# Element-wise work moved from GpSimd to VectorE, operands split in the tile they were loaded into, and one pair's scaled tokens kept, in a hybrid decoder layer

## The chip, the cores and the metric

The kernel runs on one core of a Trainium2 chip. The metric is the device time of one execution in microseconds (us). The kernel before takes 2348.49 us, the median of three runs (2345.11 to 2351.36). TensorE multiplies matrices; VectorE (DVE in the profile), ScalarE (ACT) and GpSimd (POOL) do element-wise work; SP issues nearly all transfers between HBM and the on-chip memory (SBUF). Matmul results lie in PSUM, from where VectorE or ScalarE fetch them.

## The reference

One decoder layer on 2048 tokens of width 1024, all in float32:

```python
h = modulate(rmsnorm(x, norm1_w), shift1, scale1)
x = x + gate1 * hybrid_mixer(h, ...)      # w_in, attention | state space, w_out
h = modulate(rmsnorm(x, norm2_w), shift2, scale2)
g, u = split(h @ w_gate_up)               # width 2816 each
x = x + gate2 * ((silu(g) * u) @ w_down)
return rmsnorm(x, final_norm_w)
```

`hybrid_mixer` is one input projection, then a sliding-window attention (window 128) in 8 heads beside a chunked state-space scan in 8 heads with a causal convolution before and a gated norm behind, and one output projection (`w_out`) of the two side by side. Shifts, scales and gates come from a small product of `c`.

## The kernel before, in words

*Tiling.* Activations lie transposed: features on the 128 partitions, 512 tokens (a block, `T`) along the free dimension; there are four blocks, `b` = 0 to 3. Width 1024 is 8 tiles (`KT`), 2816 is 22 (`NF`) or, in halves, 11 (`KP`).

*Two halves of every operand.* Matmuls take a 32-bit format that keeps fewer bits of the mantissa. So each operand is split: ScalarE copies it to the rounded form (`hi`), and VectorE or GpSimd subtracts that from the original (`lo`). A product is then three matmuls, hi by hi, hi by lo and lo by hi. That makes a subtraction of 128x512 elements for every weight tile and every token tile, the commonest element-wise work of the kernel. `weight` (L260) does it for projections, with an argument for the engine; `halves` (L849) for the gate and up weights; `shifted` and `kept` (L875, L880) for tokens of the feed-forward part; `tokens_of` (L1055) and the steps of `steps_of` (L1066) for the down projection. The last two alternate between VectorE and GpSimd, by counters.

*Stages.* (1) For each block: norm, projections, convolution, attention (`attentions`) and scan (`ssds`), with an output projection (`out_proj`, L808) at its end. It reads the block's eight mixed tiles, which attention and scan have left in HBM (`spill`): `mixed` (L802) loads each into a temporary tile `t` and splits it into an operand pair. Chunk c of the projection takes 24 matmuls into one PSUM bank; then L821 adds the gated result to x, which frees the bank for chunk c + 2. The projections of blocks 2 and 3 run after the first `quads`.

(2) The feed-forward part works on pairs of blocks, `s` = 0 and 1. Gate and up products are done with seven block products in place of eight: `quad` (L956) makes, from four loaded weight tiles, four sums and differences s1 to s4 (L962 to L968), splits seven weights, and multiplies them by seven prepared token operands (b11, b21, t1, b22, t3, t2, t4); some twenty adds and multiplies on the results follow, and the products go to HBM. One `quad` is 84 matmuls, and there are 22 for each `s`. `operands_last` (L930) prepares the token operands of the second pair: four tiles per k are loaded, scaled (`scaled`, L865, with its operation at L872) and combined.

(3) The down projection uses the same scheme: seven stages per pair (`pairs.stage`), each multiplying eleven token tiles (loaded ahead in a `ring` by `tokens_of`) by four chunks of weights (`steps_of`, 12 steps). Three stages of the first pair run before the second pair's quads. Four of the seven weights are sums of the down weights, made once by `weight_sums` (L1038) in 16 pieces beside the quads: four loads, two operations on VectorE, two on GpSimd, four stores.

*Order.* Every engine works through its queue in order. The program is written as generators that yield between pieces; `beside(main, ratio)` runs side work in a given share. A scheduler then sets each engine's order from a simulated timeline, except where a block fixes it for TensorE (the first part) or VectorE (the last stage). So a small edit of an engine moves neighbours too. `norm_of` issues the final norm of a finished block at steps 2 and 5 of the next stage.

*Tiles.* Split weights have 6 tiles (`SPLIT`), raw ones 5 (`RAW`), temporaries 8 (`TMP`). The eight operand pairs of an output projection, `mo`, come from one pool per block (`op` and `op3`).

Of the kernel before, what the change touches and what calls it, by code (L numbers as in the profile page):

```python
# [43 lines left out]
def hymba_layer(ctx, tc, xT, crow, pos, wada, wadk, vecs, rows, wq, wkv, wz, wx, wo, wgu, wd, outT):  # L44
# [206 lines left out]

    def split(x, into):
        hi, lo = into
        nc.scalar.activation(hi, x, AF.Copy)
        split.last = nc.vector.tensor_tensor(lo, x, hi.bitcast(F32), ALU.subtract)
        return hi, lo
# [545 lines left out]
    def mixed(b, mix, cs, into):  # L802
        for c in cs:
            m = tmp()
            nc.sync.dma_start(m, spill[b][c])
            mix.append(split(m, into(c)))

    def out_proj(b, y_of, mix, bank_of, acc, norm=None, each=lambda c: None):  # L808
        for c in range(KT):
            ps = bank_of(c)  # L810
            for half in range(2):
                if half:
                    yield
                whi, wlo = weight(wo[c, half], T, ("o", c, half), b == 0, nc.gpsimd if half or b < 2 else nc.vector, b > 1)
# [26 lines left out]

    flip = [0]

    def lower(lo, x, hi):
        flip[0] += 1
        eng = nc.vector if flip[0] % 2 else nc.gpsimd
        eng.tensor_tensor(lo, x, hi.bitcast(F32), ALU.subtract)
# [40 lines left out]
    def operands_first(s, ops, bc):  # L888

        for k in range(4):  # L890
            h = scaled(s, k, bc, ((0, 0), (1, 0)))
            shifted(ops["b11"][k], h[0, 0], shift_of(k, 0))
            shifted(ops["b21"][k], h[1, 0], shift_of(k, 1))
            yield

# [34 lines left out]
    def operands_last(s, ops, bc):  # L930

        for k in range(4):
            h = scaled(s, k, bc, ((1, 1), (0, 1), (0, 0), (1, 0)))
# [3 lines left out]
            kept(ops["t3"][k], t3)  # L937
# [4 lines left out]
            kept(ops["t2"][k], t2)  # L942
# [13 lines left out]
    def quad(s, f, ops, banks, fresh, behind):  # L956
# [5 lines left out]
        nc.gpsimd.tensor_tensor(s1, a21, a22, ALU.add)  # L962
        nc.gpsimd.tensor_tensor(s2, s1, a11, ALU.subtract)
        ws1 = halves(s1, nc.vector)
        ws2 = halves(s2, nc.gpsimd)
        nc.gpsimd.tensor_tensor(s3, a11, a21, ALU.subtract)
        ws3 = halves(s3, nc.gpsimd)
        nc.gpsimd.tensor_tensor(s4, a12, s2, ALU.subtract)  # L968
        ws4 = halves(s4, nc.gpsimd)
# [68 lines left out]
    def weight_sums(pool):  # L1038

        n = KP * P // 4  # L1040
        for c in range(4):
            for q in range(4):
# [5 lines left out]
                nc.gpsimd.tensor_tensor(a21, a21, a22, ALU.add)  # L1048
                nc.vector.tensor_tensor(a22, a22, a11, ALU.subtract)
                nc.gpsimd.tensor_tensor(a12, a12, a22, ALU.subtract)  # L1050
# [4 lines left out]
    def tokens_of(s, name, pool, n):  # L1055

        for k in range(KP):
# [4 lines left out]
            flip[0] += 1  # L1062
            (nc.vector if flip[0] % 2 else nc.gpsimd).tensor_tensor(lo, raw, hi.bitcast(F32), ALU.subtract)  # L1063
            yield hi, lo

    def steps_of(act, src, banks, new, done, ts=slice(0, T), kept_w=None):  # L1066

        turn = [0]
        for c in range(4):
# [3 lines left out]
            for lo, hi in CHUNKS:  # L1073
# [3 lines left out]
                else:  # L1077
                    turn[0] += 1
# [10 lines left out]
                    (nc.vector if turn[0] % 2 else nc.gpsimd).tensor_tensor(w[1], raw, w[0].bitcast(F32), ALU.subtract)  # L1089
# [579 lines left out]
```

## Time and profile before

| | value |
|---|---|
| median of three runs | 2348.49 us (2345.11 to 2351.36) |
| profiled execution | 2349.26 us, its span 2347.6 us |
| mean granted TensorE clock | 0.971 |
| matmuls | 11072 |
| element-wise instructions of VectorE and GpSimd | 2674 and 1287 |
| bytes read from HBM and written to it | 335.50 MB and 130.61 MB |

The page gives busy time by engine. "Idle before" in a row of a group is the time the engine stood still just before its instructions, and the name behind it is what ended that. In the waits, "A <- B: total, times, longest" says that A stood still until B was done. PEclk is the share of full clock that TensorE was granted; in stretches in which it idles the clock falls for a while and matmuls last longer, so that time is lost beyond the gap itself. A stretch such as 1240.00:1280.00 is counted from the first instruction. In time, the first part fills about 0 to 780 us, the quads of the first pair 780 to 1320, the output projections of blocks 2 and 3 about 1260 to 1440, three down stages 1440 to 1500 and beyond, the quads of the second pair from 1540, and the other eleven down stages from 1980 to the end.

### The profile page before, as it was taken

To read this page: it belongs to the slowest core of one execution; us is meant where nothing else is said; L and a number is where in the kernel's file an instruction comes from. 1 tells how busy PE (TensorE), PEld (TensorE's weight loads), DVE (VectorE), ACT (ScalarE), POOL (GpSimd) and SP (SyncE) were. 2 spreads that over 40 slices of the span, in tenths; PEclk is the share of its full clock that TensorE was granted. 3 is DMA by queue.
4 is the path that set the end of the run, shared out by engine and by line. 5 is a ranking of instruction groups with operands and counts; after the bars stand their busy time and mean duration, and the time that the engine had idled before them with its cause. 6 is when DMAs were issued, how large, how long until landed. Compare 5 with 4: busy or idle time off the path is not lost. (4 is left out here: it accounts for less than half of the span.)

```text
span 2347.6 us, 33637 instructions
## 1 busy us (share of the span) xinstructions
PE 2194.1 (93%) x11072; PEld 1817.4 (77%) x11072; DVE 1625.4 (69%) x2674; ACT 1006.1 (43%) x2113; POOL 1355.4 (58%) x1287
## 2 busy tenths in 40 slices
PE   6878989999999999999998988998999999999998
PEld 5778778888879788877876766776788888787887
DVE  8987975773568866777774658776766665676565
ACT  4564543654346555333333434442233333544442
POOL 2556433553223845687783636887766665765572
PEclk9998999999999999999998999998999999999999
DMA  8898887777879432433333567766432324867653
GB/s 296 294 325 298 301 255 247 253 248 249 297 265 313 148 100 82 126 99 109 112 113 114 188 219 265 274 217 216 152 108 95 108 95 147 294 228 245 197 178 112
DMA packets 288174, 468.36 MB, mean 200 GB/s; under 512 B 27264, under 2 KB 96896, under 8 KB 288000
## 3 DMA queue, kind: packets, MB, share of 16 engines
q1 hardware_dynamic: 287424, 465.70, 59.4%
q8 instruction: 87, 1.43, 0.3%
q14 instruction: 87, 0.71, 0.1%
q10 hardware_dynamic: 576, 0.52, 0.1%
HBM read 335.50 MB, written 130.61 MB: 199 GB/s over the span
## 5 line engine op out<-in xcount | busy, mean ns | idle before, releaser
L1093 PE MATMUL d<-a,w 128*128 128x512 f32 x1716 | 412.6, 401 | 15.9 <-POOL a L1063 5.2
L1093 PEld LDWEIGHTS d<-a,w 128*128 128x128 f32 x1716 | 326.9, 191 | 98.6 <-POOL a L1063 5.6
L952 PE MATMUL d<-b,w 128*128 128x512 f32 x924 | 367.6, 401 | 7.2 <-ACT t L975 5.8
L954 PE MATMUL d<-b,w 128*128 128x512 f32 x924 | 370.1, 402 | 3.5 <-POOL w L853 2.0
L953 PE MATMUL d<-b,w 128*128 128x512 f32 x924 | 369.5, 400 | 0.3 <-POOL b L883 0.3
L952 PEld LDWEIGHTS d<-b,w 128*128 128x128 f32 x924 | 176.0, 190 | 48.4 <-ACT t L975 6.9
L954 PEld LDWEIGHTS d<-b,w 128*128 128x128 f32 x924 | 175.9, 190 | 44.9 <-POOL w L853 3.2
L852 ACT ACTIVATE w<-s 128x512 fp32r<-128x512 f32 x176 | 110.8, 632 | 226.7 <-PE d L954 167.2
L953 PEld LDWEIGHTS d<-b,w 128*128 128x128 f32 x924 | 176.2, 191 | 40.7 <-POOL b L883 0.7
L853 POOL TENSOR_TENSOR w<-s,w 128x512 fp32r<-128x512 f32 x132 | 190.6, 1446 | 15.7 <-ACT w L852 11.6
L276 PE MATMUL d<-w,hl 128*128 128x256 f32 (+1 forms) x592 | 176.6, 298 | 8.6 <-ACT hl L327 6.4
L278 PE MATMUL d<-w,hl 128*128 128x256 f32 (+1 forms) x592 | 171.9, 290 | 2.0 <-DVE hl L328 2.0
L277 PE MATMUL d<-w,hl 128*128 128x256 f32 (+1 forms) x592 | 171.9, 290 | 0.0
L1089 POOL TENSOR_TENSOR w<-raw,w 128x512 fp32r<-128x512 f32 (+1 forms) x78 | 112.8, 1449 | 86.8 <-ACT w L1088 86.7
L968 POOL TENSOR_TENSOR s<-raw,s 128x512 f32<-128x512 f32 x44 | 58.8, 1337 | 174.3 <-DVE w L853 86.7
L286 POOL TENSOR_TENSOR acc<-acc,t 128x512 f32<-128x512 f32 x70 | 99.2, 1417 | 98.4 <-ACT t L285 98.0
L269 POOL TENSOR_TENSOR w<-raw,w 128x512 fp32r<-128x512 f32 (+1 forms) x68 | 94.7, 1394 | 97.8 <-ACT w L268 89.2
L853 DVE TENSOR_TENSOR w<-raw,w 128x512 fp32r<-128x512 f32 x132 | 138.3, 1050 | 17.7 <-ACT w L852 16.6
L276 PE MATMUL d<-hl,w 128*128 128x512 f32 x352 | 147.2, 418 | 3.2 <-ACT w L268 2.2
L1063 DVE TENSOR_TENSOR a<-a 128x512 fp32r<-128x512 f32 x77 | 104.5, 1372 | 62.7 <-ACT a L1061 56.7
L278 PE MATMUL d<-hl,w 128*128 128x512 f32 x352 | 141.2, 401 | 1.4 <-DVE w L269 0.7
L277 PE MATMUL d<-hl,w 128*128 128x512 f32 x352 | 140.7, 400 | 0.0
(417 smaller groups left out, 5532.0 us busy)
## 6 DMA issues: line engine op xcount, KB each, us to landing
raw<-in_wgu_dram SPq DMA_DIRECT2D x176, 256.0 KB, 2.8
w<-w_x SPq DMA_DIRECT2D x48, 512.0 KB, 5.2
act_t<-t SPq DMA_DIRECT2D x88, 256.0 KB, 2.3
a<-act_t SPq DMA_DIRECT2D x88, 256.0 KB, 5.2
t<-in_xT_dram SPq DMA_DIRECT2D x80, 256.0 KB, 4.1
act_b<-t SPq DMA_DIRECT2D x66, 256.0 KB, 2.1
a<-act_b SPq DMA_DIRECT2D x66, 256.0 KB, 5.1
aw<-in_wada_dram SPq DMA_DIRECT2D x64, 256.0 KB, 4.3
```

What stands on the lines that cost most here:

```text
L276: nc.tensor.matmul(out, ahi, bhi, start=first, stop=False)
L277: nc.tensor.matmul(out, ahi, blo, start=False, stop=False)
L278: mm3.last = nc.tensor.matmul(out, alo, bhi, start=False, stop=last)
L286: eng.tensor_tensor(acc, acc, sq, ALU.add)
L852: nc.scalar.activation(hi, x, AF.Copy)
L853: eng.tensor_tensor(lo, x, hi.bitcast(F32), ALU.subtract)
L952: nc.tensor.matmul(out, ahi, bhi, start=first and k == 0, stop=False, skip_group_check=True)
L953: nc.tensor.matmul(out, ahi, blo, start=False, stop=False, skip_group_check=True)
L954: mm3.last = nc.tensor.matmul(out, alo, bhi, start=False, stop=k == 3, skip_group_check=True)
L1063: (nc.vector if flip[0] % 2 else nc.gpsimd).tensor_tensor(lo, raw, hi.bitcast(F32), ALU.subtract)
L1089: (nc.vector if turn[0] % 2 else nc.gpsimd).tensor_tensor(w[1], raw, w[0].bitcast(F32), ALU.subtract)
L1093: mm3.last = nc.tensor.matmul(ps, w[x][:, ws], act[k][y][:, ts], start=new and k == 0 and x + y == 0, stop=k == KP - 1 and x == 1, skip_gr ...
```

## The change

It has six parts. (a) VectorE takes over from GpSimd: the sums of `quad` (s3 and s4 only for the first pair), all splits of its weights, all splits of tokens and weights in the down projection, the weight sums, the second halves of `wo` in the last two output projections, and two of the four kept operands in `operands_last`. (b) `mixed` loads into the `lo` half of the operand tile and splits there, without a temporary. (c) The operand pairs of blocks 2 and 3 share one ring of 11 tiles; three of block 3's tiles are loaded as block 2's projection nears its end, the other five at the start of block 3's. (d) `operands_first` of the second pair stores its eight scaled tiles in HBM, and `operands_last` loads them instead of loading and scaling again. (e) Tokens for the stage after the last quads are loaded four steps earlier. (f) The final norm is issued at steps 6 and 9.

```diff
     def mixed(b, mix, cs, into):
         for c in cs:
-            m = tmp()
+            hi, lo = into(c)
+            m = lo.bitcast(F32)
             nc.sync.dma_start(m, spill[b][c])
-            mix.append(split(m, into(c)))
+            nc.scalar.activation(hi, m, AF.Copy)
+            nc.vector.tensor_tensor(lo, m, hi.bitcast(F32), ALU.subtract)
+            mix.append((hi, lo))
...
-                whi, wlo = weight(wo[c, half], T, ("o", c, half), b == 0, nc.gpsimd if half or b < 2 else nc.vector, b > 1)
+                whi, wlo = weight(wo[c, half], T, ("o", c, half), b == 0, nc.gpsimd if b < 2 else nc.vector, b > 1)
...
             h = scaled(s, k, bc, ((0, 0), (1, 0)))
+            if s:
+                for i in range(2):
+                    nc.sync.dma_start(scaled_d[i][k], h[i, 0])
...
     def operands_last(s, ops, bc):
...
-            h = scaled(s, k, bc, ((1, 1), (0, 1), (0, 0), (1, 0)))
+            h = {}
+            for i in range(2):
+                h[i, 0] = tmp()
+                nc.sync.dma_start(h[i, 0], scaled_d[i][k])
+            h.update(scaled(s, k, bc, ((1, 1), (0, 1))))
...
-            kept(ops["t3"][k], t3)
+            kept(ops["t3"][k], t3, nc.vector)
...
-            kept(ops["t2"][k], t2)
+            kept(ops["t2"][k], t2, nc.vector)
...
-        nc.gpsimd.tensor_tensor(s1, a21, a22, ALU.add)
-        nc.gpsimd.tensor_tensor(s2, s1, a11, ALU.subtract)
+        nc.vector.tensor_tensor(s1, a21, a22, ALU.add)
+        nc.vector.tensor_tensor(s2, s1, a11, ALU.subtract)
         ws1 = halves(s1, nc.vector)
-        ws2 = halves(s2, nc.gpsimd)
-        nc.gpsimd.tensor_tensor(s3, a11, a21, ALU.subtract)
-        ws3 = halves(s3, nc.gpsimd)
-        nc.gpsimd.tensor_tensor(s4, a12, s2, ALU.subtract)
-        ws4 = halves(s4, nc.gpsimd)
+        ws2 = halves(s2, nc.vector)
+        other = nc.gpsimd if s else nc.vector
+        other.tensor_tensor(s3, a11, a21, ALU.subtract)
+        ws3 = halves(s3, nc.vector)
+        other.tensor_tensor(s4, a12, s2, ALU.subtract)
+        ws4 = halves(s4, nc.vector)
...
-                nc.gpsimd.tensor_tensor(a21, a21, a22, ALU.add)
+                nc.vector.tensor_tensor(a21, a21, a22, ALU.add)
...
-                nc.gpsimd.tensor_tensor(a12, a12, a22, ALU.subtract)
+                nc.vector.tensor_tensor(a12, a12, a22, ALU.subtract)
...
-            (nc.vector if flip[0] % 2 else nc.gpsimd).tensor_tensor(lo, raw, hi.bitcast(F32), ALU.subtract)
+            nc.vector.tensor_tensor(lo, raw, hi.bitcast(F32), ALU.subtract)
...
-                    (nc.vector if turn[0] % 2 else nc.gpsimd).tensor_tensor(w[1], raw, w[0].bitcast(F32), ALU.subtract)
+                    nc.vector.tensor_tensor(w[1], raw, w[0].bitcast(F32), ALU.subtract)
...
-    def loaded(b, c, pool):
-        mixed(b, mixes[b], (c,), lambda c: pair("mo", KT, pool=pool))
+    def loaded(b, c):
+        mixed(b, mixes[b], (c,), lambda c: pair("mo", 11, pool=op))
...
-        yield from output(2)
+        yield from output(2, lambda c: loaded(3, c - 5) if c > 4 else None)
...
-        for c in range(KT):
-            loaded(3, c, op3)
+        for c in range(3, KT):
+            loaded(3, c)
...
-        next(second)
         for i, _ in enumerate(first):
             if i % 2:
                 next(coming, None)
+        next(second)
...
-            if i >= 7 * NF - 12:
+            if i >= 7 * NF - 16:
                 next(coming, None)
...
-                if i in (2, 5):
+                if i in (6, 9):
                     for b in list(finish_of):
                         norm_of(b)
```

The order in which instructions stand moves with it. Lines of the changed kernel are up to ten smaller (L853 becomes L843, L255 becomes L802, L821 becomes L818, L269 becomes L263).

GpSimd's queue at the end of the state-space scan, before. `rss`, `rs` and `ss` belong to the reciprocal root of the scan's gated norm, `s` are weight sums of a quad:

```order
L269 TENSOR_TENSOR w<-raw,w 128x512
L962 TENSOR_TENSOR s<-raw 128x512
L240 TENSOR_SCALAR rss<-ss 128x2
L242 TENSOR_TENSOR rss<-rs 128x2
L963 TENSOR_TENSOR s<-s,raw 128x512
L966 TENSOR_TENSOR s<-raw 128x512
L243 TENSOR_TENSOR rss<-rss 128x2
L244 TENSOR_SCALAR rss<-rss 128x2
L245 TENSOR_TENSOR rs<-rss,rs 128x2
```

and in the change:

```order
L1011 TENSOR_TENSOR t<-t 128x512
L756 TENSOR_TENSOR m_12997<-m_12997,m_12844 128x512
L240 TENSOR_SCALAR rss<-ss 128x2
L242 TENSOR_TENSOR rss<-rs 128x2
L243 TENSOR_TENSOR rss<-rss 128x2
L244 TENSOR_SCALAR rss<-rss 128x2
L1005 TENSOR_TENSOR t<-t 128x512
L245 TENSOR_TENSOR rs<-rss,rs 128x2
```

The sums and a split have left the chain of the root; one addition of a quad's results (L1005) stands in it instead. In TensorE's queue the transposes of that block's result (L715, now L709) stood 5 products behind the last state product and directly ahead of the first `mo` matmul; they now stand 48 products behind the one and 42 ahead of the other.

VectorE's queue at the output projections of blocks 2 and 3, before. `mo` are split mixed tokens, `w` low halves of `wo`, `at` and `am` the two PSUM banks:

```order
L269 TENSOR_TENSOR w<-raw,w 128x512
L255 TENSOR_TENSOR mo<-t,mo 128x512 x3
L269 TENSOR_TENSOR w<-raw,w 128x512
L255 TENSOR_TENSOR mo<-t,mo 128x512 x5
L821 SCALAR_TENSOR_TENSOR t<-at,mod,t 128x512
L821 SCALAR_TENSOR_TENSOR t<-am,mod,t 128x512
```

and in the change, at the last two chunks of block 2:

```order
L818 SCALAR_TENSOR_TENSOR t<-am,mod,t 128x512
L263 TENSOR_TENSOR w<-raw,w 128x512
L802 TENSOR_TENSOR mo<-mo 128x512
L263 TENSOR_TENSOR w<-raw,w 128x512
L818 SCALAR_TENSOR_TENSOR t<-at,mod,t 128x512
L802 TENSOR_TENSOR mo<-mo 128x512
L263 TENSOR_TENSOR w<-raw,w 128x512
L802 TENSOR_TENSOR mo<-mo 128x512 x3
L263 TENSOR_TENSOR w<-raw,w 128x512 x2
```

Eight splits stood ahead of an eviction; five now stand around the last one, and three further up.

VectorE's queue in a quad of the second pair beside the weight sums (`ws`), before:

```order
L1047 TENSOR_TENSOR ws<-ws 128x352
L853 TENSOR_TENSOR w<-s,w 128x512
L1004 TENSOR_TENSOR t<-t,st 128x512
L1049 TENSOR_TENSOR ws<-ws 128x352
L1008 TENSOR_TENSOR t<-t,sm 128x512
L1010 SCALAR_TENSOR_TENSOR t<-t 128x512
```

and in the change:

```order
L1047 TENSOR_TENSOR ws<-ws 128x352
L843 TENSOR_TENSOR w<-s,w 128x512
L1048 TENSOR_TENSOR ws<-ws 128x352
L1004 TENSOR_TENSOR t<-t,st 128x512
L843 TENSOR_TENSOR w<-s,w 128x512
L1049 TENSOR_TENSOR ws<-ws 128x352
L961 TENSOR_TENSOR s<-raw 128x512
L1050 TENSOR_TENSOR ws<-ws 128x352
L843 TENSOR_TENSOR w<-s,w 128x512
L962 TENSOR_TENSOR s<-s,raw 128x512
L1008 TENSOR_TENSOR t<-t,sm 128x512
```

Between the evictions of two products (L1004 and L1008) there stood one sum; now two sums, two splits and two sums of the quad's own stand there.

More of the change, by code (lines that the diff above doesn't have):

```diff
@@ L250, in rsqrt @@
             nc.vector.scalar_tensor_tensor(y, b, 1.5, y, ALU.add, ALU.mult)
[L252 to L256, printed above, removed]
     split_d = {}
@@ L840, in hymba_layer @@
     held = {}
[L842 to L847, printed above, removed]
     def halves(x, eng):
@@ L894, in operands_first @@
             yield
+    scaled_d = [[dr.tile([P, T], F32, name=f"scaled{i}{k}") for k in range(4)] for i in range(2)]
     def operands_between(s, ops, bc):
@@ L1061, in tokens_of @@
             nc.scalar.activation(hi, raw, AF.Copy)
-            flip[0] += 1
-            (nc.vector if flip[0] % 2 else nc.gpsimd).tensor_tensor(lo, raw, hi.bitcast(F32), ALU.subtract)
+            nc.vector.tensor_tensor(lo, raw, hi.bitcast(F32), ALU.subtract)
             yield hi, lo
     def steps_of(act, src, banks, new, done, ts=slice(0, T), kept_w=None):
-        turn = [0]
         for c in range(4):
@@ L1077, in steps_of @@
                 else:
-                    turn[0] += 1
                     n = (hi - lo) * P
@@ L1514, in output @@
         yield from out_proj(b, y_of, mixes[b], lambda c: side_bank(c % 2), sums(op), lambda: side_bank(2), each)
-    def loaded(b, c, pool):
-        mixed(b, mixes[b], (c,), lambda c: pair("mo", KT, pool=pool))
+    def loaded(b, c):
+        mixed(b, mixes[b], (c,), lambda c: pair("mo", 11, pool=op))
     def first_output():
         for c in range(KT):
-            loaded(2, c, op)
+            loaded(2, c)
             if c % 2:
                 yield
-        yield from output(2)
+        yield from output(2, lambda c: loaded(3, c - 5) if c > 4 else None)
     def second_output():
-        for c in range(KT):
-            loaded(3, c, op3)
+        for c in range(3, KT):
+            loaded(3, c)
         yield
@@ L1554, in hymba_layer @@
         act, coming = ring(0, "b11", dn, KP)
-        op3 = outputs.enter_context(tc.tile_pool(name="op3", bufs=1, side="right", reuse_waits="tile"))
         second = second_output()
-        next(second)
         for i, _ in enumerate(first):
```

## The prediction

> **What bounds the kernel now.** I read the first part of the page, the busy times by stretch, the waits of TensorE, and last the order of instructions at the longest waits.
>
> ```profile
> PE 2194.1 (93%) x11072; PEld 1817.4 (77%) x11072; DVE 1625.4 (69%) x2674; ACT 1006.1 (43%) x2113; POOL 1355.4 (58%) x1287
> ```
>
> TensorE is busy for 93%, but not always at full speed. The view by stretches shows where it loses time:
>
> ```profile
> core 0 of [0], span 2347.6 us
> core 0: us, PE busy (x) PEld busy (x) DVE busy (x) ACT busy (x) POOL busy (x), PEclk, DMA share, GB/s
> 780.00:1240.00 460.00, 447.81 (x2159) 366.34 (x2158) 331.30 (x471) 191.43 (x438) 319.91 (x303) 0.99 0.33 106
> 1240.00:1280.00 40.00, 28.97 (x114) 22.78 (x113) 18.58 (x28) 16.66 (x34) 16.47 (x24) 0.83 0.32 95
> 1340.00:1380.00 40.00, 29.25 (x121) 23.23 (x121) 21.12 (x39) 13.65 (x23) 13.99 (x11) 0.87 0.66 221
> 1440.00:1500.00 60.00, 48.22 (x182) 36.67 (x181) 57.33 (x53) 29.76 (x54) 55.29 (x36) 0.89 0.75 256
> 1560.00:1700.00 140.00, 124.64 (x504) 97.91 (x503) 99.15 (x102) 38.09 (x67) 103.13 (x75) 0.94 0.59 187
> 1740.00:1920.00 180.00, 180.00 (x777) 145.85 (x777) 109.16 (x121) 59.63 (x101) 119.48 (x85) 1.00 0.31 103
> 2010.00:2044.00 34.00, 29.86 (x120) 22.93 (x119) 21.67 (x20) 16.05 (x31) 24.52 (x17) 0.95 0.71 245
> 2105.00:2140.00 35.00, 32.34 (x136) 25.66 (x135) 25.11 (x41) 14.65 (x27) 19.74 (x14) 0.95 0.62 197
> ```
>
> The profiled execution took 2349.26 us, its span of 2347.6 and 1.66 around it; the median of the timed runs is 2348.49, near enough that the sum below, made against 2349.3, needs no correction.
>
> From 1740 to 1920 us nothing disturbs TensorE: 777 matmuls in 180 us, 0.2317 us each at clock 1.00. By that pace the other stretches should have taken their count times 0.2317 us. They lose 40 - 26.4 = 13.6 us at 1240; 40 - 28.0 = 12.0 at 1340; 60 - 42.2 = 17.8 at 1440; 140 - 116.8 = 23.2 at 1560; 34 - 27.8 = 6.2 at 2010; and about 4.5 at 2105, where a few of the 136 matmuls are small. That is 77 us, idle time and the slow clock behind it (0.83 at 1240) together. The waits of TensorE from 1240 to 2140 us name the engines in charge (total, times, longest):
>
> ```profile
> PE at L276 <- DVE t L821: 10.2, 1, 10.2
> PE am L954 <- DVE w L853: 7.0, 2, 3.5
> PE st L715 <- ACT m L794: 6.8, 1, 6.8
> PE d L952 <- ACT t L975: 5.8, 2, 4.7
> PE d L1093 <- POOL a L1063: 5.2, 1, 5.2
> PE d L1093 <- DVE w L1089: 4.5, 2, 3.8
> PE am L276 <- ACT mo L254: 4.3, 1, 4.3
> PE sm L291 <- POOL acc L286: 2.7, 1, 2.7
> ```
>
> TensorE mostly waits for low halves and for evictions. From 1440 to 1500 us VectorE (57.33 of 60) and GpSimd (55.29) are both full. And they stretch each other; groups of VectorE from 1740 to 1920 us:
>
> ```profile
> L853 DVE TENSOR_TENSOR w<-raw,w 128x512 fp32r<-128x512 f32 x27 | 27.5, 1017 | 2.2 <-ACT w L852 1.6
> ...
> L1015 DVE TENSOR_TENSOR t<-t 128x512 f32<-128x512 f32 x5 | 8.9, 1784 | 0.0
> L853 DVE TENSOR_TENSOR w<-s,w 128x512 fp32r<-128x512 f32 x10 | 6.9, 689 | 1.6 <-ACT w L852 1.6
> ```
>
> one with an input in PSUM, from 780 to 1240 us, and GpSimd's commonest in the whole span:
>
> ```profile
> L1008 DVE TENSOR_TENSOR t<-t,d 128x512 f32<-128x512 f32 x19 | 13.0, 686 | 28.5 <-PE d L954 28.3
> ```
>
> ```profile
> L853 POOL TENSOR_TENSOR w<-s,w 128x512 fp32r<-128x512 f32 x132 | 190.6, 1446 | 15.7 <-ACT w L852 11.6
> ```
>
> One and the same subtraction takes 0.69 us where it falls clear of GpSimd's work (`w<-s,w`), 1.02 in the mean where it sometimes doesn't, and an operation that always starts beside GpSimd 1.78. One whose second input lies in PSUM (L1008) stays at 0.686. So it is the two inputs from SBUF that collide.
>
> **The change, part by part.** *Moved to VectorE:* by the order, 481 operations leave GpSimd: L853 132, L962 and L963 88, L966 and L968 of the first 22 quads 44, L1089 84, L1063 77, weight sums 32, second halves of `wo` 16, two of the four kept operands 8. At 0.69 us each VectorE gains at most 332 us and loses 8 scalings and part of its stretching; GpSimd loses some 481 x 1.45 = 697. Where TensorE sets the pace, as from 1740 to 1920, this is worth nothing.
>
> *End of the state-space work (1240, 13.6 us).* L715 waits for a scaling by a reciprocal root that GpSimd computes in small operations, with quad work between them:
>
> ```profile
> 1245.13 1.27 POOL L962 TENSOR_TENSOR s<-raw 128x512 f32<-128x512 f32 x1
> 1246.38 0.18 POOL L240 TENSOR_SCALAR rss<-ss 128x2 f32<-128x2 f32 x1
> 1246.72 0.19 POOL L242 TENSOR_TENSOR rss<-rs 128x2 f32<-128x2 f32 x1 [0.16 <-DVE rs L238]
> 1247.08 1.26 POOL L963 TENSOR_TENSOR s<-s,raw 128x512 f32<-128x512 f32 x1 [0.16 <-POOL rss L242]
> 1248.30 1.71 POOL L966 TENSOR_TENSOR s<-raw 128x512 f32<-128x512 f32 x1
> ```
>
> These three big ones, 4.2 us of the 6.8 waited, go. And the changed TensorE order puts 48 products (11 us) ahead of these transposes and 42 behind them, ahead of the first `mo` matmul, which covers the rest and the 4.3 us. Bounds 0 and 13.6; I take 10, near the upper end, since both causes go.
>
> *Fourth block's mixed tokens (1340, 12.0 us).* L821, which frees the PSUM bank, stands in VectorE's queue behind eight splits that wait for loads:
>
> ```profile
> 1352.38 0.69 DVE L255 TENSOR_TENSOR mo<-t,mo 128x512 fp32r<-128x512 f32 x1 [2.21 <-ACT mo L254]
> ...
> 1357.97 0.74 DVE L821 SCALAR_TENSOR_TENSOR t<-at,mod,t 128x512 f32<-128x512 f32 x1
> ```
>
> The loads of these tokens, with their median time to landing:
>
> ```profile
> t<-mix SPq DMA_DIRECT2D x32, 256.0 KB, 5.5
> ```
>
> Now three of the eight are split ahead, and the eviction of the last chunk but one stands before the other five. What is late next: those five reuse tiles of the third block and can only be loaded while its last chunk is multiplied. The first tile is free after 3 of that chunk's 24 matmuls and wanted 9 into the next chunk: 30 x 0.23 = 6.9 us for a landing of 5.5, an ACT pass and a split of 0.69. That is just about even, so a few us of a wait may stay. Bounds 0 and 12; I take 7. For the other blocks, splitting in the loaded tile leaves loads and operations as many as they were, each load only bound to its operand tile: -3 to +3 us, taken as 0.
>
> *Operands of the second pair (1440, 17.8 us).* Of GpSimd's 36 operations there, 28 go: these, with 8 of the 16 L883, and four sums.
>
> ```profile
> L883 POOL TENSOR_TENSOR b<-t,b 128x512 fp32r<-128x512 f32 x16 | 25.5, 1607 | 6.8 <-DMA raw<-in_wd_dram 5.5 <-ACT b L882 1.3
> L1063 POOL TENSOR_TENSOR a<-a 128x512 fp32r<-128x512 f32 x8 | 13.2, 1663 | 0.7 <-ACT a L1061 0.6
> L1089 POOL TENSOR_TENSOR w<-raw,w 128x512 fp32r<-128x512 f32 (+1 forms) x8 | 12.7, 1586 | 0.0
> ```
>
> VectorE's 53 lose 8 scalings, which become loads, and gain 28: 73 x 0.69 = 50 us, against 57 now; TensorE needs 42. Unless work slides to the neighbours the stretch shrinks to VectorE's 50, so by 10; bounds 0 and 17.8; I take 9. The eight stores of scaled tokens are new on SP's queue, the eight reads replace eight reads; hidden behind the stages between them, 0. Were one landing exposed, it would be 5.5 by the row above.
>
> *Weight sums (1560, 23.2 us).* The move cuts both ways here. VectorE already waits for their loads (1440 to 1680 us), and what stands behind in its queue waits too:
>
> ```profile
> L1047 DVE TENSOR_TENSOR ws<-ws 128x352 f32<-128x352 f32 x15 | 14.2, 948 | 24.8 <-DMA ws<-in_wd_dram 24.8
> ```
>
> So far GpSimd could go on splitting summed weights meanwhile; now all seven splits of a quad stand in the one queue. Against that, splits and sums shorten toward 0.69 and 0.52, and the sums no longer pass from engine to engine. Weights are made a quad ahead (84 matmuls, 19 us), longer than a landing. Bounds 0 and 23.2; I take 10, below the middle.
>
> *Down stages.* Tokens of the next stage loaded four steps earlier at the end of the quads, and one engine for all low halves: between 0 and 6.2 us at 2010, taken as 3.5. The norm's matmuls, set back from steps 2 and 5 to 6 and 9, stand 28 matmuls (6.5 us) later, more than the 2.7 waited at L291; the clock of 0.95 over 35 us is 1.8 more: 4 of the 4.5 at 2105. The Trainium skill ("TensorE: Matmul & The Clock Gate", section "HAM oscillation — how this bites in real kernels") lets the clock fall only after idle gaps above about 3.4 us; by it this wait would return 2.7 and the sum come to 40.2. The row shows 0.95 around a gap of 2.7, so I keep 4.
>
> *New load in the first quads (780 to 1240):* the four sums and three splits of 19 quads, 133 operations or 92 us, on VectorE's 331 of 460. Part of its stretching goes with them. Bounds: the 12 us of TensorE's idle time there won, or rival 1's 53 lost; I set 2 lost, because its queue keeps slack.
>
> ```profile
> L968 POOL TENSOR_TENSOR s<-raw,s 128x512 f32<-128x512 f32 x19 | 26.1, 1372 | 74.5 <-DVE w L853 37.8 <-issue 36.0 <-POOL s L966 0.7
> ```
>
> Sum: 10 + 7 + 9 + 10 + 3.5 + 4 - 2 = 41.5; 2349.3 - 41.5 = 2307.8, say **2308 us**.
>
> **Rivals.** (1) *VectorE becomes the bound of the first quads, and the kernel is slower.* 331 + 92 = 423 us of 460 if no stretching goes. VectorE also stands idle for 129 us there, 28.3 of them for TensorE at L1008. Were 90 of those kept, 513 us, 53 more than now; with 43.5 won elsewhere the time is 2359. It decides from some 504 us on. Against it: with GpSimd's share more than halved some of the 331 must fall, and part of that idle time is mere lack of work. Chance 0.12. The Trainium skill ("Perfetto Trace Analysis", section "Optimizing Scalar/DVE Operations") speaks for it: it would relieve a saturated DVE by GpSimd, not the reverse, and warns that shifting work between these two may not help, since they share a port. The 1.78 us row bears out the port.
>
> (2) *The waits are only changed.* VectorE, waiting for loads of the sums and of the five mixed tiles, holds up the weights behind them, so that 1340, 1440 and 1560 give a third of their 26: 2349.3 - 8.7 - 10 - 7.5 + 2 = 2325. For it: the 24.8 us above. Chance 0.20.
>
> (3) *No change:* each removed wait is taken up by the next dependence of TensorE on VectorE; 2349. Against it: the order shows work between the waits and what ended them. Chance 0.08.
>
> (4) *All 77 us go:* 2272. The 50 us of VectorE against 42 of TensorE at 1440 speak against it. Chance 0.10.
>
> **How the numbers follow.** The forecast holds 0.50, by itself 2290 to 2322. A measurement of this kernel tells about 0.3% (7 us) from no change. Forecast, (2) and (4) are faster: 0.80; (3) is the same: 0.08; (1) slower: 0.12. The range 2275 to 2345 leaves out (1), half of (3) and the lower part of (4).
>
> **What would show it.** Right: the waits of 10.2 us at the output projection and 6.8 at the transposes are gone; the splits of the undisturbed quads fall from 1.02 to 0.7 to 0.8 us while L1008 stays at 0.69; GpSimd falls below 30% of the span and VectorE stays near 1650 us, because less stretching pays for the new work; 1440 to 1500 loses half as much. Wrong: TensorE waits more for VectorE between 780 and 1240 us (rival 1), or the stretch of the sums still loses 20 us with VectorE idle for `ws` (rival 2).

## The result, and the profile after

The changed kernel takes 2267.61 us in the median of four runs (2266.14 to 2270.63), beside 2349.93 us of the kernel before on the same chip (2345.11 to 2351.49): a ratio of 0.9655, 95% interval 0.9637 to 0.9673. It is 82 us faster where 41.5 were predicted, and 7 us below the lower end of the range. The profiled span went from 2347.6 to 2265.4 us.

The first part of the page, after:

```profile
PE 2166.4 (96%) x11072; PEld 1801.9 (80%) x11072; DVE 1681.7 (74%) x3147; ACT 1008.4 (45%) x2113; POOL 700.2 (31%) x806
```

GpSimd lost 481 operations and half of its busy time. VectorE has 473 more and is busy for only 56 us more. The view by stretches, with the same columns as before:

```profile
744.00:1195.00 451.00, 447.25 (x2210) 368.33 (x2209) 366.16 (x621) 208.74 (x474) 146.65 (x179) 1.00 0.37 116
1195.00:1241.00 46.00, 46.00 (x203) 37.42 (x202) 34.76 (x57) 22.50 (x45) 14.29 (x18) 1.00 0.51 169
1281.00:1341.00 60.00, 58.96 (x257) 47.37 (x256) 43.60 (x74) 28.84 (x51) 14.61 (x9) 1.00 0.78 259
1351.00:1463.00 112.00, 107.15 (x457) 84.78 (x457) 94.45 (x155) 53.30 (x94) 29.14 (x14) 1.00 0.91 307
1463.00:1620.00 157.00, 150.69 (x635) 121.00 (x635) 129.38 (x190) 52.68 (x92) 44.08 (x29) 0.98 0.67 216
2019.00:2054.00 35.00, 35.00 (x157) 28.46 (x156) 22.84 (x47) 16.75 (x31) 6.52 (x3) 1.00 0.59 187
```

The clock is at 0.98 to 1.00 in all these rows, and TensorE has no gap at the end of the state-space scan (1195 to 1241). By 0.2317 us a matmul, 6.1 us are still lost from 1351 to 1463 and 9.9 from 1463 to 1620. The waits of TensorE from 750 to 2230 us:

```profile
PE d L951 <- ACT t L975: 4.4, 2, 3.9
PE d L1090 <- DVE a L1062: 3.9, 4, 1.5
PE am L271 <- DVE m L661: 2.4, 1, 2.4
...
PE at L270 <- DVE t L818: 1.0, 1, 1.0
```

Of the wait of 10.2 us (now L270 for L818) 1.0 is left; that of 6.8 at the transposes is gone.

To see where the 82 us came from, I took the same point of work in each trace, the n-th of the 11072 matmuls, and compared when it starts. Each row is the stretch up to such a matmul, named by its time before, in us gained over the kernel before:

| up to matmul (time before) | predicted | after | splits in the tile alone | moves alone | both |
|---|---|---|---|---|---|
| 4257 (752, the first quad product) | 0 | 8.2 | 10.4 | 3.2 | 3.7 |
| 6427 (1214) | -2 | 16.7 | 1.5 | 16.8 | 17.0 |
| 6663 (1281) | 10 | 15.2 | 14.6 | 15.2 | 15.1 |
| 7172 (1412) | 7 | 10.7 | 4.1 | 5.6 | 10.3 |
| 7584 (1527) | 9 | 13.6 | -0.5 | -0.5 | 2.1 |
| 9443 (1982) | 10 | 13.9 | -1.0 | 9.2 | 10.3 |
| 10163 (2159) | 7.5 | 8.1 | 3.2 | 6.9 | 6.9 |
| the end (2348) | 0 | -4.2 | 0.0 | -3.7 | -2.7 |
| sum | 41.5 | 82.2 | 32.3 | 52.7 | 62.7 |

The last three columns belong to experiments below. Single profiles differ in the first row: eleven kernels whose code up to that point is that of the change reach it between 741.2 and 750.9 us. The later rows are differences within one trace, but they too move by 3 to 5 us with mere order, as one experiment below shows. And the trace of the kernel before is of an execution of 2349.26 us, 3 to 6 us above its medians in the experiments, so that a part of each column may be no gain at all.

### The profile page after: what moved, and what is told of

Its sections match the earlier page's. It is cut to its first block, busy times and chain, and to the rows that moved or that the text cites. A ratio compares the mean times of both kernels' runs of the same rounds, so it can differ in the third digit from the quotient of the medians.

```text
span 2265.4 us, 33515 instructions
## 1 busy us (share of the span) xinstructions
PE 2166.4 (96%) x11072; PEld 1801.9 (80%) x11072; DVE 1681.7 (74%) x3147; ACT 1008.4 (45%) x2113; POOL 700.2 (31%) x806
## 5 line engine op out<-in xcount | busy, mean ns | idle before, releaser
L1090 PE MATMUL d<-a,w 128*128 128x512 f32 x1716 | 405.6, 396 | 7.0 <-DVE a L1062 3.9
L1090 PEld LDWEIGHTS d<-a,w 128*128 128x128 f32 x1716 | 321.6, 188 | 87.8 <-DVE a L1062 5.7
L280 POOL TENSOR_TENSOR acc<-acc,t 128x512 f32<-128x512 f32 x70 | 106.2, 1518 | 404.4 <-ACT t L279 389.8
L270 PE MATMUL d<-w,hl 128*128 128x256 f32 (+1 forms) x592 | 175.8, 297 | 6.9 <-ACT hl L321 4.5
L270 PE MATMUL d<-hl,w 128*128 128x512 f32 x352 | 146.3, 416 | 4.3 <-ACT w L262 2.2
L843 DVE TENSOR_TENSOR w<-s,w 128x512 fp32r<-128x512 f32 x176 | 143.2, 815 | 8.6 <-ACT w L842 7.3
L1086 DVE TENSOR_TENSOR w<-raw,w 128x512 fp32r<-128x512 f32 x156 | 107.2, 696 | 53.6 <-ACT w L1085 53.4
L842 ACT ACTIVATE w<-raw 128x512 fp32r<-128x512 f32 x132 | 82.9, 630 | 130.4 <-PE d L953 59.1
L1085 ACT ACTIVATE w<-raw 128x512 fp32r<-128x512 f32 x156 | 90.7, 588 | 102.7 <-PE d L1090 67.5
L1005 POOL TENSOR_TENSOR t<-t 128x512 f32<-128x512 f32 x44 | 75.3, 1712 | 180.5 <-DVE t L1004 124.1
```

Of the source, the lines that this page charges most:

```text
L270: nc.tensor.matmul(out, ahi, bhi, start=first, stop=False)
L280: eng.tensor_tensor(acc, acc, sq, ALU.add)
L1086: nc.vector.tensor_tensor(w[1], raw, w[0].bitcast(F32), ALU.subtract)
L1090: mm3.last = nc.tensor.matmul(ps, w[x][:, ws], act[k][y][:, ts], start=new and k == 0 and x + y == 0, stop=k == KP - 1 and x == 1, skip_gr ...
```

## The experiments

All times are medians beside the kernel before on the same chip in the same job; its medians there lay between 2343.72 and 2346.49 us, below the 2349.93 beside the changed kernel. So a difference of a few us between medians of two jobs shows little; the ratios hold within a job.

**One part alone.** The kernel before with (b) only, with (a) only, and with both and nothing of (c) to (f). (a) is those lines of the diff above that name another engine. For (b) alone the whole edit is

```
-            m = tmp()
+            hi, lo = into(c)
+            m = lo.bitcast(F32)
             nc.sync.dma_start(m, spill[b][c])
-            mix.append(split(m, into(c)))
+            nc.scalar.activation(hi, m, AF.Copy)
+            nc.vector.tensor_tensor(lo, m, hi.bitcast(F32), ALU.subtract)
+            mix.append((hi, lo))
```

> Kernel before, with one part of the change alone: mixed tokens are loaded into the low half of the operand tile and split there. Theory A (the part removes a wait near 480 us, where two splits stood ahead of the scan's decays): 3.1 + 0.9 us of waits and about 3 us of slow clock go, so the first quad starts some 7 to 8 us earlier and the time is about 2342 us; nothing else changes. Theory B (those 8 us of the whole change came from elsewhere, for instance from temporaries set free): the first quad starts within 2 us of before, 2349 us.

> Kernel before, with all 481 operations moved from GpSimd to VectorE and nothing else of the change. Theory A (what cost time was that the two engines held each other up): the first quads gain 11, the end of the state-space work 20, the second pair's operands 15, the weight sums 14, the down stages 4, in all 64 us, 2286 us; the 10 us wait of the output projection and the 2.7 us wait at the norm stay. Theory B (the new tiles and loads were needed for most of it): at least 2320 us.

> The kernel before with parts (a) and (b) together and nothing of (c) to (f). Alone they gained 26 and 49 us, but both removed the same loss of about 21 us at the end of the state-space scan. Theory A, that loss can be won once, and (c) to (f) supply the rest of the 82: 2286 to 2297. Theory B, (a) and (b) do it all: 2268 to 2274.

(b) alone: 2318.04 us, ratio 0.9881 (0.9852 to 0.9910), below both theories. (a) alone: 2295.35, 0.9782 (0.9753 to 0.9810), nearer theory A. Both: 2282.92, 0.9732 (0.9716 to 0.9748), theory A.

The wait near 480 us that theory A for (b) names is there, and it does shrink. Before, with two stretched splits of mixed tokens ahead of the scan's decays in VectorE's queue:

```profile
PE st L742 <- DVE m L731: 3.1, 1, 3.1
PE sm L704 <- DVE m L737: 0.9, 1, 0.9
```

```profile
479.47 3.46 DVE L255 TENSOR_TENSOR hl<-t,hl 128x512 fp32r<-128x512 f32 x2
```

and with (b) alone, where the splits ahead of the decays, now of L808, take 0.69 us each:

```profile
PE st L742 <- DVE m L731: 2.0, 1, 2.0
```

```profile
472.40 0.69 DVE L808 TENSOR_TENSOR hl<-hl 128x512 fp32r<-128x512 f32 x1 [0.51 <-ACT hl L807]
474.34 0.69 DVE L808 TENSOR_TENSOR hl<-hl 128x512 fp32r<-128x512 f32 x1 [1.25 <-ACT hl L807]
```

From the 2584th to the 2771st matmul (475 to 505 us before) thirteen of the fourteen traces with (b) gain 3.9 to 5.0 us, the fourteenth, with nearly all splits on VectorE, 1.5; (a) alone gains 1.4, and the kernel before with some loads moved 0.6.

But "nothing else changes" does not hold. The sum of the two gains, 75 us by medians, is not reached (64) mainly because each alone gains the whole 15 us at the end of the state-space scan. For (b) that cannot come from the chain of the reciprocal root. GpSimd's timeline there, with (b) alone:

```profile
1232.69 1.28 POOL L965 TENSOR_TENSOR s<-raw 128x512 f32<-128x512 f32 x1 [3.26 <-DMA raw<-in_wgu_dram]
1233.93 0.19 POOL L240 TENSOR_SCALAR rss<-ss 128x2 f32<-128x2 f32 x1
1234.08 0.19 POOL L242 TENSOR_TENSOR rss<-rs 128x2 f32<-128x2 f32 x1
1234.23 1.30 POOL L966 TENSOR_TENSOR s<-s,raw 128x512 f32<-128x512 f32 x1
1235.49 1.29 POOL L969 TENSOR_TENSOR s<-raw 128x512 f32<-128x512 f32 x1
1236.74 0.64 POOL L243 TENSOR_TENSOR rss<-rss 128x2 f32<-128x2 f32 x1
1237.34 1.30 POOL L269 TENSOR_TENSOR w<-raw,w 128x512 fp32r<-128x512 f32 x1
...
1239.74 1.29 POOL L1008 TENSOR_TENSOR t<-t 128x512 f32<-128x512 f32 x1
```

The big operations still stand between the small ones, and yet TensorE no longer waits at the transposes. What changed is TensorE's order: 53 products now lie between the last state product and the transposes and 48 between these and the first `mo` matmul, where the kernel before has 5 and none. From the last state product to the transposes 12.1 us pass, against 7.9 before: nothing shows a shorter chain, work covers it. With (a) alone the counts are 48 and 30, in the changed kernel 48 and 42. Why the scheduler places the transposes later after either edit is not settled.

**The first quads.** The changed kernel with the sums and the three splits of the first pair's quads back on GpSimd:

```
+        first = nc.vector if s else nc.gpsimd
-        nc.vector.tensor_tensor(s1, a21, a22, ALU.add)
+        first.tensor_tensor(s1, a21, a22, ALU.add)
...      (s2 and the splits of s2, s3, s4 alike; s3 and s4 on GpSimd)
```

> Changed kernel, with the sums and summed-weight splits of the first 22 quads back on GpSimd, as before the change. Theory A (this move gave the 31 us between the first quad and the last transposes of the scan): about 2268 + 31 = 2299 us, with a wait of 5 to 7 us at the transposes again. Theory B (those gains come from the order, which is made anew by any edit): less than 10 us are given back, 2268 to 2278 us. Theory C (VectorE is close to its limit there and the move costs something that the rest won back): faster than 2268 us.

Measured 2281.88, ratio 0.9719 (0.9689 to 0.9750), 14 us lost; between theories A and B, nearer B. The gain up to 1214 us falls from 16.7 to 1.5, which is all of the loss; the trace is of the fastest of its four executions (2275.43). The gain at the end of the scan, which theory A had go as well, stays at 14.1, although the sums stand in the chain of the root again: here too the transposes lie far behind, 51 products on one side and 50 on the other. TensorE's waits in the first quads, before:

```profile
PE sm L780 <- DVE m L709: 4.6, 3, 2.1
PE st L768 <- DVE m L761: 3.5, 2, 2.0
PE am L585 <- DVE ast L638: 2.6, 1, 2.6
```

and with these operations back on GpSimd:

```profile
PE sm L774 <- DVE m L703: 4.6, 3, 2.1
PE st L762 <- DVE m L755: 3.5, 2, 2.0
PE am L579 <- DVE ast L632: 1.2, 1, 1.2
```

So without this part of (a) the waits are back, 9.3 of 10.7 us. In the changed kernel all three are gone; from 780 us on a wait of 1.2 for ScalarE (L701) is the only one left. They belong to attention and scan, not to the quads. L709 (now L703) is an SBUF operation of that chain, and it took 1362 ns here before and takes 847 now:

```profile
L709 DVE TENSOR_TENSOR m<-m,m 128x512 f32<-128x512 f32 x14 | 19.1, 1362 | 1.5 <-ACT m L707 1.5
```

```profile
L703 DVE TENSOR_TENSOR m<-m,m 128x512 f32<-128x512 f32 x16 | 13.6, 847 | 4.2 <-ACT m L701 4.2
```

The other two operations did not become shorter: L761 (now L755), which reads PSUM, took 681 ns and takes 686, and L638 (now L632) 477 and 478. They must start earlier. Whether that is because those ahead of them in VectorE's queue are shorter, or because the queue's order is another, no run here tells apart.

**More of the same move.** The changed kernel with all remaining quad work on VectorE as well, then with nearly all splits of projection weights and all kept operands too:

```
-        other = nc.gpsimd if s else nc.vector
+        other = nc.vector
-        nc.gpsimd.tensor_tensor(c22, c22, u3, ALU.add)
+        nc.vector.tensor_tensor(c22, c22, u3, ALU.add)
-        nc.gpsimd.tensor_tensor(g2, g2, c22, ALU.mult)
+        nc.vector.tensor_tensor(g2, g2, c22, ALU.mult)
```

> The changed kernel with all remaining work of the quads moved to VectorE too: s3 and s4 of the second pair, and the two GpSimd operations on results in every quad, 132 operations at 0.69 us or 91 us more on VectorE, over some 900 us in which it is now busy for about 75%. Theory A, VectorE still has room, and what is left of the stretching goes: 2258 to 2268, its pure SBUF subtractions at 0.69. Theory B, VectorE becomes the bound of the quads, or its queue holds evictions up: 2275 or more, with TensorE waiting for VectorE between 750 and 1200 us and from 1460 on.

```
-    def weight(src, n, key, store, eng=nc.gpsimd, fresh=False):
+    def weight(src, n, key, store, eng=nc.vector, fresh=False):
...      (the calls for the halves of wx and wo alike)
-    def kept(into, x, eng=nc.gpsimd):
+    def kept(into, x, eng=nc.vector):
```

> The kernel with all quad work on VectorE, with in addition all splits of projection weights and all kept operands on VectorE, some 72 more subtractions, most of them before 750 us, where VectorE is busy for 548 us of 744. Theory A, stretching falls there too: 2245 to 2254. Theory B, the first part is bound by chains and loads, not by GpSimd's splits: 2255 to 2260. Theory C, VectorE's queue holds the chains up there: 2262 or more.

The first: 2257.17 us, ratio 0.9621 (0.9604 to 0.9639), theory A. Its page, with 605 operations more on VectorE than before for 62.6 us more busy time:

```profile
PE 2165.4 (96%) x11072; PEld 1803.1 (80%) x11072; DVE 1688.0 (75%) x3279; ACT 1011.2 (45%) x2113; POOL 503.9 (22%) x674
```

From 780 to 1190 us no wait of TensorE is listed at all. VectorE's groups from 1660 to 1860 us, in the changed kernel:

```profile
L843 DVE TENSOR_TENSOR w<-raw,w 128x512 fp32r<-128x512 f32 x30 | 25.1, 837 | 5.7 <-ACT w L842 5.6
L961 DVE TENSOR_TENSOR s<-raw 128x512 f32<-128x512 f32 x11 | 17.7, 1606 | 1.0
```

and where GpSimd has no quad work left:

```profile
L843 DVE TENSOR_TENSOR w<-raw,w 128x512 fp32r<-128x512 f32 x32 | 22.1, 690 | 8.1 <-ACT w L842 7.0 <-DMA act_t<-t 0.9
...
L961 DVE TENSOR_TENSOR s<-raw 128x512 f32<-128x512 f32 x10 | 6.8, 684 | 0.0
```

All lengthening is gone: 0.69 us for each. Beside the changed kernel it gains 6.6 us more in the second pair's quads (20.5). The second kernel, 2265.22 (0.9648, 0.9599 to 0.9697), fits theory C by its median, but its interval takes in the first one's, so that a loss is not shown. In its trace, of the fastest of its four executions (2260.44), the start gains 1 us, within the scatter, and the second pair's quads fall back to 16.2.

**The kept scaled tokens.** The changed kernel without (d), and the same with the residual's loads of two down stages put ahead:

```
-            h = {}
-            for i in range(2):
-                h[i, 0] = tmp()
-                nc.sync.dma_start(h[i, 0], scaled_d[i][k])
-            h.update(scaled(s, k, bc, ((1, 1), (0, 1))))
+            h = scaled(s, k, bc, ((1, 1), (0, 1), (0, 0), (1, 0)))
```

> The changed kernel without part (d): the second pair's first tokens are neither stored nor read back, but loaded and scaled again on VectorE in operands_last. Between the last first-pair product and the first second-pair product (1340 to 1530 us of the kernel before) the change gained 24.3 us, the splits alone lost 4.7 there and the moves alone gained 5.1. Theory A, the kept scaled tokens gain what is missing: 2283 +- 4, that stretch 15 to 20 us longer than in the changed kernel. Theory B, the stretch is won by splits and moves together and (d) is worth its eight VectorE operations at most: 2268 to 2274.

```
+            if name in ("b21", "t4") and not self.pool:
+                for c in range(2):
+                    self.residual(int(name == "t4"), 0, c)
...
-                    self.residual(i, 0, c)
+                    if (i, 0, c) not in self.x:
+                        self.residual(i, 0, c)
...
+                        if c < 2:
+                            self.residual(i, 0, c + 2)
```

> The kernel without part (d), in which TensorE stood still for 13.9 us at 1430 us, with one edit: in the two down stages beside the token operands, the first two loads of the residual are issued before the stage begins, and each later one when the second before it is used. Before, they stood behind eleven loads of the next stage's tokens in SP's queue. Theory A, (d) gains because it moves these loads ahead: the stop at 1430 us is gone and the time comes to 2269 to 2276. Theory B, (d) gains because VectorE has eight scalings less: the stop stays, 2283 to 2289.

Without (d): 2286.49, ratio 0.9747 (0.9731 to 0.9762). By the number (d) is worth 19 us, as theory A had it. By the trace 15 are lost in the row up to 1527 and 8 in the second pair's quads behind it, and both come back with the second edit. Of the 15, 14 are one stop of TensorE, at a down stage:

```profile
PE d L1083 <- DVE t L1114: 13.9, 1, 13.9
```

L1114 adds the product to the residual, which L1098 loads. SP's queue without (d):

```profile
1425.21 1.33 SPq L1053 DMA_DIRECT2D a<-act_t  x3
...
1433.85 0.80 SPq L1053 DMA_DIRECT2D a<-act_t  x2
1434.84 0.32 SPq L1045 DMA_DIRECT2D wd_s<-ws  x1
1435.49 0.33 SPq L1039 DMA_DIRECT2D ws<-in_wd_dram  x1
1436.26 0.32 SPq L1098 DMA_DIRECT2D t<-mid  x1
```

Eleven loads of the next stage's tokens, spread over 9 us, stand ahead of the residual. In the changed kernel, with (d), its first two loads stand ahead of them:

```profile
1421.39 0.79 SPq L1105 DMA_DIRECT2D t<-mid  x2
...
1423.87 0.43 SPq L1060 DMA_DIRECT2D a<-act_t  x1
```

With two of the residual's loads put ahead and no (d), the queue reads

```profile
1414.31 0.33 SPq L1098 DMA_DIRECT2D t<-mid  x1
...
1416.07 0.32 SPq L1098 DMA_DIRECT2D t<-mid  x1
...
1422.13 1.61 SPq L1053 DMA_DIRECT2D a<-act_t  x2
```

the stop is gone, the stretch up to 1527 gains 11.1 in place of -1.5, and the time is 2266.68 (0.9653, 0.9611 to 0.9694), 2 us below theory A's range: as good as the changed kernel's, though no scaled tokens are kept. So (d) gains by the place it gives these loads, and the eight scalings and reads are worth nothing that can be measured. Is the wait an old one?

> The kernel before with one edit: in the two down stages beside the token operands the residual's first two loads are issued before the stage, each later one two chunks ahead. Theory A, the kernel before did not wait for these loads (its stops there, 5.2 and 3.8 us, end on GpSimd's a and VectorE's w), and the wait of 14 us only comes with the moves: 2342 to 2350, no change. Theory B, it lost there too by their place: 2330 to 2338.

The same edit in the kernel before: 2341.51, ratio 0.9982 (0.9964 to 1.0000), no change, as theory A had it, with 1.4 us lost in the stretch that ends at 1527. The old waits there ended on GpSimd's `a` and VectorE's `w`. In this kernel, in which nothing but the place of a few loads is changed, the rows up to 1214, 1982 and 2159 gain 3.0, 5.0 and 3.8 by the trace, while the medians differ by 2.8 in all. It is the moves that bring the new wait: 14.8 us with (a) alone, 13.6 with (a) and (b).

> All quad work on VectorE, part (d) left out, and the residual's loads ahead instead. Theory A, the kept scaled tokens are worth nothing once these loads are in place: 2254 to 2260, as with the kept tokens (2257). Theory B, eight scalings less on VectorE do count where it has all the quads' work: 2262 or more.

With all quad work on VectorE, the loads ahead and no kept tokens: 2257.15, ratio 0.9618 (0.9587 to 0.9650), theory A, the same as with the kept tokens.

**Smaller parts.** Block 2 and 3 with two sets of tiles as before (c undone), the weight sums' two operations back on GpSimd, and the down projection's splits alternating again:

```
-        mixed(b, mixes[b], (c,), lambda c: pair("mo", 11, pool=op))
+        mixed(b, mixes[b], (c,), lambda c: pair("mo", KT, pool=pool))
...      (the second pool and the place of block 3's loads as before)
```

> Changed kernel, with two separate sets of eight operand tiles for the output projections of blocks 2 and 3 and the loads of block 3 issued as before the change. Theory A (the ring of 11 is what removed the wait of 10 us at the bank's eviction): 8 to 10 us are given back, 2276 us, with one wait of about 10 us between two chunks. Theory B (VectorE freed of the collisions would have been in time anyway): 2268 us, no wait over 3 us there.

```
-                nc.vector.tensor_tensor(a21, a21, a22, ALU.add)
+                nc.gpsimd.tensor_tensor(a21, a21, a22, ALU.add)
...      (a12 alike)
```

> The changed kernel with the weight sums' two operations back on GpSimd, the other two on VectorE. In the second pair's quads the change gained 13.9 us. Theory A, as in the prediction, the sums on one engine are what gained there: 10 to 14 us return, 2277 to 2282. Theory B, it is the splits and sums of the quads themselves, and the weight sums are worth little: 2266 to 2271.

```
-            nc.vector.tensor_tensor(lo, raw, hi.bitcast(F32), ALU.subtract)
+            flip[0] += 1
+            (nc.vector if flip[0] % 2 else nc.gpsimd).tensor_tensor(lo, raw, hi.bitcast(F32), ALU.subtract)
...      (the weights of steps_of alike, by the same counter)
```

> The changed kernel with the splits of tokens and weights of the down projection alternating between VectorE and GpSimd as before. Theory A, one engine for them is what gained the 8 us of the last stages and, with less stretching, part of the 1350 to 1460 us stretch: 2275 to 2285, with waits of TensorE for GpSimd's a or w returning. Theory B, earlier loads and the other parts did it: 2266 to 2271.

(c) undone: 2272.80, ratio 0.9690 (0.9653 to 0.9727), 5 us by medians and 8 by ratios, between its theories. The row up to 1412, where (c) acts, keeps 10.0 of its 10.7; what is lost is lost in the second pair's quads. TensorE's wait for L818 at the output projections comes back as 2.9 us, not as 10.2; with (b) alone it is 5.8, with (a) alone 5.2, with both 2.5. Weight sums: 2275.51, 0.9695 (0.9651 to 0.9738), 8 us, nearer theory A by the number. But by the trace, of the slowest of its four executions, 5.6 fall in the row up to 1527, where the first sums run, and only 2.1 in the second pair's quads, where theory A had 10 to 14. Down splits: 2284.09, 0.9730 (0.9687 to 0.9773), 16 us, theory A by the number: 16.1 lie in the row up to 1527 and only 2.5 in the last stages. Not by its cause: TensorE waits 0.8 us for GpSimd's `a` from 1340 to 1480 us, and its longest wait there is again for late token loads, 9.8 us; SP issues all eleven only from 1434.11 us on, and TensorE stands still until 1443.55:

```profile
PE d L1094 <- ACT a L1063: 11.6, 2, 9.8
```

**The end.**

> The changed kernel with the norm of the last stage at steps 2 and 5 as before, 6 and 9 in all others. The changed kernel lost 4 to 5 us behind its 1300th late matmul. Theory A, the norm's later place in the last stage did it: 2263 +- 1.5, and the gap before the sum of squares (1.58 us) gone. Theory B, the loss belongs to the moved engines of the last steps (the moves alone, with the norm at 2 and 5, show 3.7 there as well): 2267 +- 1.5.

The edit is `if i in ((2, 5) if is_last else (6, 9))`. Measured 2267.02, ratio 0.9662 (0.9648 to 0.9677), theory B: the norm's steps are not what cost 4 us.

> The same as e19_all_vector_loads_ahead, but in the last down stage alone the splits of weights alternate between VectorE and GpSimd as before. The changed kernel lost 3.5 to 5 us behind its 1500th late matmul. Theory A, this stage's splits on VectorE delay the last additions and the norm: 3 us below e19_all_vector_loads_ahead. Theory B, the loss is elsewhere: within 1.5 us of it.

The edit sends every second weight split of the last stage to GpSimd: `eng = nc.gpsimd if kept_w is not None and turn[0] % 2 == 0 else nc.vector`. Measured 2255.45, ratio 0.9609 (0.9571 to 0.9648): the medians differ by 1.7 us, less than they scatter, which decides between neither theory. By the traces, the last 300 matmuls take 40.5 us before, 45.4 in the changed kernel, 45.3 in the one this is an edit of and 42.1 here, so this accounts for some 3 us of the loss. The kernel with all splits of the down projection alternating agrees: it loses 0.4 us at the end in place of 4.2.

The kernels with all quad work on VectorE are about 10 us faster than the changed one by medians and 8 by ratios; the intervals of the ratios (0.9604 to 0.9639 and 0.9637 to 0.9673) just touch. No run takes (e) away by itself, and none (f) from the stages before the last.

## Why the prediction was right and wrong

The direction was right, and so was the collision it started from: operations with two inputs from SBUF stretch, and taking GpSimd out shortens VectorE's. The 1.02 us of `w<-raw,w` fell to 0.84 in the undisturbed quads (0.7 to 0.8 predicted) and L1008 stayed at 0.69; GpSimd fell to 31% (below 30% predicted) and VectorE rose to 1682 us (1650 predicted). The size was half of what was measured, 41 us short. By terms:

- *New load in the first quads, -2:* this step failed most; it gained 16.7, beyond its upper bound of 12, and is 18.7 of the 41 us. Rival 1 and this term charged 0.69 us for each operation added. Over the same 2170 matmuls busy time rose by only 22 us for 139 operations (338.98 to 361.22 us), since what was already there shortened, and the waits that went were those of the attention and scan chains for VectorE, 10.7 us; the other 6 are slow clock behind them, by the difference. VectorE is busy for 366 us of 451 there, far from the 504 of rival 1, which is refuted. I had asked how full its queue would be, not which engine ended the waits of TensorE there.
- *End of the state-space work, 10:* 15.2, above the upper bound of 13.6. One cause was wrong. Behind the new order of TensorE the three big operations in the root's chain are worth nothing: with (b) alone, and again with the first quads' sums back on GpSimd, they are still there, and nearly the whole gain is too (14.6 and 14.1). The order suffices; what taking them out would gain under the old order no run shows.
- *Splitting in the loaded tile, 0:* wrong. Alone it gained 26 us by medians, 14.6 by that order in its trace. It moves no operation between engines, but it moves TensorE's queue, which I had read only for the change as a whole. It also gains some 5 us at 480 us, at the scan of an earlier block: most of the 8.2 in the first row, for which the prediction had nothing. The fourteen traces with (b) reach the first quad product at 745.7 us in the mean, three without at 752.0.
- *Fourth block's mixed tokens, 7:* 10.7, near the upper end, but by other parts. I gave the term to (c); (a) and (b) bring 5.6 and 4.1, together 10.3, without it.
- *Operands of the second pair, 9:* 13.6, and the sum by VectorE's total was not what decided. (a) and (b) together bring 2.1 there. The "0" for the loads of (d) on SP's queue was the missed step: the moves bring a wait of 14 us for the residual's loads, and (d) removes it again by changing SP's order.
- *Weight sums, 10:* the second pair's quads gained 13.9; VectorE's waits for loads held up little, and rival 2 is refuted. But the sums are little of it: back on GpSimd, they cost 2.1 there, while (a) without the other parts gains 9.2 and all quad work on VectorE 20.5. It is mostly the quads' own operations.
- *Down stages, 3.5 and 4:* 8.1 measured, near the 7.5. The 3.5 at 2010 came as 3.8, and (a) alone gains as much without the earlier loads of (e). But the 4 at 2105 do not come from the norm's later steps, so that this size was right by luck: with (a) and (b) alone, the norm at steps 2 and 5, 4.4 are gained and no wait at that place is listed, and the kernel before with nothing but the residual's loads moved gains 4.0 there. So weighing the Trainium skill's clock rule ("TensorE: Matmul & The Clock Gate", section "HAM oscillation — how this bites in real kernels") against the 0.95 row changed nothing by which the sum could be judged. A stretch with (b) alone bears on the rule itself: the granted clock is 0.75 behind a wait of only 1.5 us, which eight small matmuls (128x2) follow, so here a gap well below the rule's was enough.

```profile
2090.00:2096.00 6.00, 5.18 (x20) 4.28 (x21) 6.00 (x4) 2.72 (x6) 5.84 (x4) 0.75 0.24 69
```

- *The end, 0:* 4.2 us were lost, by the traces some 3 of them to the last stage's splits on VectorE.
- *Rivals:* of the 77 us that I listed, 61.5 went (the five rows from 1281 to 2159), 18 more than the 43.5 that I took; rival 4 came close in time (2272), though by adding what it did not count: the start and the first quads, 24.9 us. What I held against it, 50 us of VectorE against 42 of TensorE at 1440, did not bind.

## What to carry to other kernels

When operations of two engines lengthen each other, as they do here, price an operation that moves by what it lengthens on both sides, not by its own duration: here 605 operations cost VectorE 63 us. Ask also whose waits the engine ends in that stretch: in the first quads it was the chains of attention and scan that gained. Where a scheduler sets the order, every edit also reorders queues, and at 1240 and 1430 us that was worth some 14 us each; compare TensorE's and SP's order around the longest waits for every part of a change by itself. Before crediting a part with a gain, see whether a mere change of place of the late load does the same.

## What was not expected of the hardware

In these kernels VectorE's total hardly rose with what it took over from GpSimd: 1625.4 us for 2674 operations before, 1681.7 for 3147 in the change, 1695.4 for 3343 with nearly all on VectorE, some 0.1 us for each one added, where one alone takes 0.69. The down projection's token splits show it best, half of them on GpSimd before, all on VectorE after:

```profile
L1063 DVE TENSOR_TENSOR a<-a 128x512 fp32r<-128x512 f32 x77 | 104.5, 1372 | 62.7 <-ACT a L1061 56.7 <-PE d L1093 5.7
```

```profile
L1062 DVE TENSOR_TENSOR a<-a 128x512 fp32r<-128x512 f32 x154 | 107.5, 720 | 37.3 <-ACT a L1061 37.0
```

Twice the operations take 3 us more. The Trainium skill's suggestion to relieve VectorE by GpSimd ("Perfetto Trace Analysis", section "Optimizing Scalar/DVE Operations") points the other way here: (a) alone, which relieves GpSimd by VectorE, gained 49 us. Of the same section's warning, that the two share a port and that shifting work between them might not help, the traces bear out the first half: the splits above take 1372 ns with GpSimd at work on the others and 720 where it does none of them.
